# Gated DeltaNet recurrence: the decay to a chunk's end moved from the new values to two copies of the keys, with two buffers each for the keys

## The chip, the cores and the metric

One core of one Trainium2 chip. The metric is the device time of one execution in microseconds (us); the kernel before takes 2288.92 us (median of three runs, 2286.33 to 2290.3).

## The reference

A decoder trunk of two layers over 1024 tokens of width 1024, in float32: layer 0 mixes a dilated attention and a gated linear recurrence, layer 1 is a gated DeltaNet. The change lies in layer 1 alone. Its core, per head, in chunks of tokens (the reference uses 64, the kernel 128):

```python
decay  = exp(where(causal, gcum[:, None] - gcum[None, :], -inf))
sol    = triangular_solve(I + strict_lower((k*b) @ k.T * decay), [v*b, k*b*exp(gcum)])
u, w   = sol                                     # w multiplies the state
q_dec  = q * exp(gcum)
k_tail = k * exp(gcum[-1] - gcum)                # the decay to the chunk's end
g_last = exp(gcum[-1])
def step(state, n):
    v_new = u[n] - w[n] @ state
    o     = q_dec[n] @ state + (q @ k.T * decay)[n] @ v_new
    state = state * g_last[n] + k_tail[n].T @ v_new
    return state, o
```

There are 8 key heads and 16 value heads; two value heads, e = 0 and 1, share one key head and differ in `gcum`. `k` and `q` come from a projection (1024 x 1024 per group), a causal convolution of 4 taps and SiLU. The output goes through an RMS norm, a SiLU gate and an output projection.

## The kernel before, in words

The kernel is written with a framework that places semaphores, gives tiles their buffers and orders each engine's instructions itself: an instruction is put in the queue of its engine when, in the order in which the program writes things, it is the first whose operands and buffers are there. So what stands later in the program can run earlier when what stands before it waits. A tile with a tag shares `bufs` slots with all tiles of that tag; a new tile gets a slot when the last reader of the slot's tile before has run.

Layer 1 (`odd_layer`) goes through eight key heads `hh`. Each has three parts:

- *Projection* `proj(j)`: first `way_out(j - 2)`, the gates of the head before (L143 to L145 into banks named oz, output through tiles `oy`, tag "oy", 2 buffers), then four convolutions `conv`: k of head j + 1 (matmuls into banks pk), the two value heads of head j (pv), q of head j (pq). Every product of the projections is three matmuls (high and low parts). A convolution takes PSUM banks of the tag "pj" (2 banks), one for each half of the tokens. ACT copies the bank to the staging tile `ub` (L822, tag "ub", 1 buffer); then the result tile (`kT`, `vT` or `q`) is taken and written by ACT (L825), worked on by DVE three times (L827), by ACT (L830) and by DVE (L831). `kT` has the tag "kT" with 3 buffers, `q` the tag "q" with 2.
- `turn_k(j)` turns the keys by PE transposes into banks "a" and copies them to `kn` (L877, tag "kn", 3 buffers), one half by ACT, one by DVE. `turn_v` does the same for the values, scaled (`bv`).
- *Inversion* `invert(hh)`: the matrix of each chunk (kk, from `kT`) is inverted on DVE in small steps (L1007, L1009) and by small matmuls; the result is `U`.
- *Recurrence* `recur(hh)`, 8 chunks of 128 tokens, both value heads side by side (2 x 128 columns). Per chunk: `ks` = keys times state (L1105), `r` = values minus that (DVE, L1108); `qs` = queries times state (L1111), `oq` = that scaled (ACT, L1114); `vp` = U times r (L1120), the new values; `vt` = vp times the decay to the chunk's end, `etl` (DVE, L1123); `vn` = plain copy of vp (ACT, L1125); `kv` = turned keys times vt (L1129); the new state `S` (DVE, L1133); `op` = attention times vn (L1140); for the next chunk `qk` (L1091) and its masked product `A` (DVE, L1093), with decays that SP loads and POOL and ACT prepare (L1079, L1081). PSUM: tag "b" has two banks, "d" one, "c" one, "a" two. `ks`, `kv` and `op` take "b"; `qs`, `vp` and `qk` take "d".

The three parts run together. While recurrence hh runs, the inversion of hh + 1 and `proj(hh + 1)` are laid between its steps:

```python
for hh in range(8):
    fill = proj(hh + 1) if hh < 7 else seq(way_out(6), gate7(), out_last(range(3), ["pj"]))
    if hh < 7:
        fill = blend(invert(hh + 1), fill, 0.8)
    mix(recur(hh), fill, 2.8)
    drain(fill)
```

So during recurrence hh the keys `kT` of three heads are about: hh (recurrence), hh + 1 (inversion), hh + 2 (being convolved). The weights come by SP's DMAs and are cut into high and low parts by ACT and DVE (L112, L113). After the last head, the output projection adds into `hr` (L273), and `after` computes the final norm into tiles `fo` (tag "kn"; L199, L1173) and writes them out. The first group of its inputs sits in the slots of "kT" and "kn" too.

Of the kernel before, what the change touches and what calls it, by code (L numbers as in the profile page):

```python
# [9 lines left out]
F32 = mybir.dt.float32  # L10
F32R = mybir.dt.float32r
# [3 lines left out]
ALU = mybir.AluOpType  # L15
# [3 lines left out]
P = 128  # L19
D = 1024  # L20
T = 1024
NT = T // P
# [56 lines left out]
def trunk_kernel(ctx: ExitStack, tc: tile.TileContext, x, ew, ewo, ow, owab, owo, nw, fnw, lbl, hnw,  # L79
                 cw, dtb, alog, onw, cst, out):  # L80
    nc = tc.nc
    dve, act, pe, pool = nc.vector, nc.scalar, nc.tensor, nc.gpsimd
# [8 lines left out]
    def bank(tag, shape, name):  # L91
        return pp.tile(shape, F32, name=name, tag=tag, bufs=BANKS[tag])
# [647 lines left out]
    def odd_layer(es):  # L740
        sp = es.enter_context(tc.tile_pool(name="od", bufs=1))
        gt = {n: sp.tile([P, NT, 16], F32, name=f"g_{n}") for n in ("beta", "gc", "ngc", "eg", "nbeg", "etl", "egl")}
# [70 lines left out]
        KT, KN, SC, Q, BV, CQ, SS, VT, US = {}, {}, {}, {}, {}, {}, {}, {}, {}  # L813
# [32 lines left out]


        def k_tile(j):
            KT[j] = sp.tile([P, T], F32, name=f"kT{j}", tag="kT", bufs=3)
            return KT[j]  # L850

        def q_tile(j):
# [9 lines left out]
        def turn_k(j):  # L862
            ss = sp.tile([P, NT], F32, name=f"kss{j}", tag="kss", bufs=2)
            tps = turn_qk(KT[j], ss, f"tk{j}")
            rn = sp.tile([P, NT], F32, name=f"rn{j}", tag="rn", bufs=2)
            tm = sp.tile([P, NT], F32, name=f"rt{j}", tag="rt", bufs=2)
            dve.tensor_scalar(ss, ss, 4.0 * EPS, None, op0=ALU.add)
            rsqrt(rn, ss, tm)

            dve.tensor_tensor(tm, rn, rn, op=ALU.mult)  # L870
            sc = SC[j] = sp.tile([P, 3, NT, 2], F32, name=f"sc{j}", tag="sc", bufs=3)
            for i, (n, f, x) in enumerate((("beta", 1.0, tm), ("nbeg", 1.0, tm), ("beta", 0.5, rn))):
                dve.scalar_tensor_tensor(sc[:, i], gt[n][:, :, 2 * j:2 * j + 2], f, x[:, :, None].to_broadcast([P, NT, 2]),
                                         op0=ALU.mult, op1=ALU.mult)
            kn = KN[j] = sp.tile([P, NT, 128], F32, name=f"kn{j}", tag="kn", bufs=3)
            for h in range(2):
                (dve.tensor_copy if h else act.copy)(kn[:, 4 * h:4 * h + 4, :], tps[h])  # L877


        def v_tile(j, e):  # L880
# [80 lines left out]
        def decays(hh, c, w):  # L961
            g = sp.tile([P, 2, 128], F32, name=f"gc{w}{hh}_{c}", tag=f"gc{w}", bufs=2)
            nc.sync.dma_start(g, bass.AP(tensor=gcd.tensor, offset=gcd.offset + (c * 16 + 2 * hh) * 128,
                                         ap=[[0, P], [128, 2], [1, 128]]))
            return g
# [106 lines left out]
        def recur(hh):  # L1072

            kT, kn, q, bv, U = KT[hh], KN[hh], Q[hh], BV[hh], US[hh]
            ss = SS[hh] = sp.tile([P, NT, 2], F32, name=f"oss{hh}", tag="oss", bufs=2)

            def decay_a(c):
                DA = decays(hh, c, "a")
                pool.tensor_tensor(DA, DA, MA[:, None, :].to_broadcast([P, 2, 128]), op=ALU.add)  # L1079
                for e in range(2):  # L1080
                    act.activation(DA[:, e, :], DA[:, e, :], AF.Exp, bias=gt["ngc"][:, c, 2 * hh + e:2 * hh + e + 1])  # L1081
                return DA

            def attend(c):

                DA = ahead_a.pop()
                if c < NT - 1:
                    ahead_a.append(decay_a(c + 1))
                qk = bank("d", [P, 128], f"qk{hh}_{c}")
                s = slice(c * 128, (c + 1) * 128)  # L1090
                pe.matmul(qk, kT[:, s], q[:, s], start=True, stop=True)  # L1091
                A = sp.tile([P, 2, 128], F32, name=f"A{hh}_{c}", tag="A", bufs=2)
                dve.tensor_tensor(A, qk[:, None, :].to_broadcast([P, 2, 128]), DA, op=ALU.mult)  # L1093
                return A

            ahead_a = [decay_a(0)]
            yield 1.0
            A = attend(0)
            St = None
            for c in range(NT):  # L1100
                col = [slice(2 * hh + e, 2 * hh + e + 1) for e in range(2)]
                s = slice(c * 128, (c + 1) * 128)
                if c:
                    ks = bank("b", [P, 2, 128], f"ks{hh}_{c}")
                    pe.matmul(ks, kT[:, s], St, start=True, stop=True)  # L1105
                    r_ = sp.tile([P, 2, 128], F32, name=f"r{hh}_{c}", tag="r")
                    for e in range(2):
                        dve.scalar_tensor_tensor(r_[:, e, :], ks[:, e, :], SC[hh][:, 1, c, e:e + 1],  # L1108
                                                 bv[:, c, e, :], op0=ALU.mult, op1=ALU.add)
                    qs = bank("d", [P, 2, 128], f"qs{hh}_{c}")  # L1110
                    pe.matmul(qs, q[:, s], St, start=True, stop=True)  # L1111
                    oq = sp.tile([P, 2, 128], F32, name=f"oq{hh}_{c}", tag="oq")
                    for e in range(2):
                        act.activation(oq[:, e, :], qs[:, e, :], AF.Copy, scale=gt["eg"][:, c, col[e]])  # L1114
                else:
                    r_ = bv[:, 0]
                yield 1.0
                vp = bank("d", [P, 2, 128], f"vp{hh}_{c}")
                for e in range(2):
                    pe.matmul(vp[:, e, :], U[:, 2 * c + e, :], r_[:, e, :], start=True, stop=True)  # L1120
                if c < NT - 1:
                    vt = sp.tile([P, 2, 128], F32, name=f"vt{hh}_{c}", tag="vt")
                    dve.tensor_tensor(vt, vp, gt["etl"][:, c, 2 * hh:2 * hh + 2, None].to_broadcast([P, 2, 128]), op=ALU.mult)  # L1123
                vn = sp.tile([P, 2, 128], F32, name=f"vn{hh}_{c}", tag="vn")
                act.copy(vn, vp)  # L1125
                yield 1.0
                if c < NT - 1:
                    kv = bank("b", [P, 2, 128], f"kv{hh}_{c}")
                    pe.matmul(kv, kn[:, c, :], vt, start=True, stop=True)  # L1129
                    Sn = sp.tile([P, 2, 128], F32, name=f"S{hh}_{c}", tag="S", bufs=2)  # L1130
                    if c:
                        for e in range(2):
                            dve.scalar_tensor_tensor(Sn[:, e, :], St[:, e, :], gt["egl"][:, c, col[e]],  # L1133
                                                     kv[:, e, :], op0=ALU.mult, op1=ALU.add)
                    else:
                        dve.tensor_copy(Sn, kv)
                    St = Sn
                op = bank("b", [P, 2, 128], f"op{hh}_{c}")
                for e in range(2):
                    pe.matmul(op[:, e, :], A[:, e, :], vn[:, e, :], start=True, stop=True)  # L1140
                A = attend(c + 1) if c < NT - 1 else None
                if c:
                    dve.tensor_tensor(bv[:, c], op, oq, op=ALU.add)
                else:
                    dve.tensor_copy(bv[:, c], op)
                for e in range(2):
                    jk = sp.tile([P, 128], BF16, name=f"oj{hh}_{c}_{e}", tag="jk", bufs=2)
                    act.activation(jk, bv[:, c, e, :], AF.Square, accum_out=ss[:, c, e:e + 1])
                yield 1.0
# [8 lines left out]
        def y_parts(g):  # L1158
            if g:
                return y_load(*y_tile(f"lo{g % 2}", 8 + g), g * 256)  # L1160
            yh = [sp.tile([P, T], F32R, name=f"oyh{c}", tag="kT", bufs=3) for c in range(2)]
            yl = [sp.tile([P, T], F32R, name=f"oyl{c}", tag="kn", bufs=3) for c in range(2)]
            y_load(yh, yl, 0)
            for t in range(NT):
                nc.sync.dma_start(hres(t), h1[t * 128:(t + 1) * 128, :])
            return yh, yl

        def after(t):
            o = sp.tile([P, D], F32, name=f"fo{t}", tag="kn", bufs=3)
            rs = norm_stats(hres(t), f"f{t}", sp, o, 2 if t == NT - 1 else 1)  # L1170
            m = D // 2 if t == NT - 1 else D
            for n in range(0, D, m):
                dve.scalar_tensor_tensor(o[:, n:n + m], hres(t)[:, n:n + m], rs, nwf[:, n:n + m], op0=ALU.mult, op1=ALU.mult)  # L1173
                nc.sync.dma_start(out[t * 128:(t + 1) * 128, n:n + m], o[:, n:n + m])
# [95 lines left out]
```

## Time and profile before

| | us |
|---|---|
| median of three runs | 2288.92 |
| the profiled execution | 2290.27 |
| its span | 2288.5 |
| PE busy in the span | 2171.9 |
| DVE busy | 1427.0 |
| ACT busy | 963.4 |
| POOL busy | 226.5 |

Times in the profile count from the start of the span. PE is the tensor engine's matmuls, PEld its weight loads, DVE the vector engine, ACT the scalar engine, POOL the GpSimd engine, SP the engine that issues DMAs. A row of the groups names line, engine, operation, output <- inputs, shape, count, then busy us and mean ns of one, then the idle time of the engine just before these instructions and what ended most of it. A row of a window has its length, then for each engine its busy time and count, then the granted clock of PE as a share of full speed and the DMA engines' share and rate. A row of a single tile has its count, the shortest, median and longest duration in ns, and the first and the last start in us. Layer 1 lies between about 1220 and 2150 us; a float32 matmul of the program shows as two in the trace.

### The profile page before, as it was taken

How to read it: one execution, taken by the hardware profiler on the slowest of the kernel's cores; microseconds unless marked ns; L12 is line 12 of the kernel's file. 1: busy time of each engine (PE TensorE's matmuls, PEld its weight loads, DVE VectorE, ACT ScalarE, POOL GpSimd, SP SyncE). 2: the span in 40 equal slices, each digit the busy share in tenths (PEclk: the TensorE clock that was granted, in tenths of full speed). 3: DMA queues.
4: the chain of work that ended last, by engine and by line, in shares of the span. 5: the costliest groups of instructions: out<-in, count | busy, mean ns of one | idle time of the engine just before them, and what ended most of it. 6: DMA issues, size and time to landing. Idle time of an engine off the chain costs nothing. (4 is left out here: it accounts for less than half of the span.)

```text
span 2288.5 us, 54642 instructions
## 1 busy us (share of the span) xinstructions
PE 2171.9 (95%) x22597; PEld 1809.0 (79%) x22597; DVE 1427.0 (62%) x3364; ACT 963.4 (42%) x2623; POOL 226.5 (10%) x236
## 2 busy tenths in 40 slices
PE   7999999999999999988999988989899989899998
PEld 6888888898888888866887776767777767678787
DVE  6444444444444444456777887878788877855777
ACT  5333333333333332322236663755555555544223
POOL 0000000000000000000000012131212121210000
PEclk9999999999999999999999998999999999999999
DMA  4111111113222323352323221121212121214232
GB/s 145 38 48 48 44 47 48 43 39 95 78 82 84 90 83 92 97 160 88 102 97 104 59 56 62 53 79 46 76 43 76 52 74 59 65 60 148 91 113 109
DMA packets 101864, 175.83 MB, mean 77 GB/s; under 512 B 16752, under 2 KB 34032, under 8 KB 101616
## 3 DMA queue, kind: packets, MB, share of 16 engines
q1 hardware_dynamic: 101616, 172.35, 24.2%
q8 instruction: 177, 2.90, 0.5%
q14 instruction: 71, 0.58, 0.1%
HBM read 127.07 MB, written 25.23 MB: 67 GB/s over the span
## 5 line engine op out<-in xcount | busy, mean ns | idle before, releaser
L113 DVE TENSOR_TENSOR w_lo<-raww,w_hi 128x512 fp32r<-128x512 f32 x292 | 211.9, 727 | 151.1 <-ACT w_hi L112 147.1
L112 ACT CAST w_hi<-raww 128x512 fp32r<-128x512 f32 x292 | 181.1, 620 | 270.1 <-PE op L145 68.0
L143 PE MATMUL av<-w_hi,hn_hi 128*128 128x256 f32 x512 | 149.0, 291 | 0.0
L143 PE MATMUL bi<-w_hi,hn_hi 128*128 128x256 f32 x512 | 147.0, 287 | 0.0
L144 PE MATMUL bi<-w_lo,hn_hi 128*128 128x256 f32 x512 | 145.3, 284 | 0.0
L144 PE MATMUL av<-w_lo,hn_hi 128*128 128x256 f32 x512 | 144.8, 283 | 0.0
L145 PE MATMUL bi<-w_hi,hn_lo 128*128 128x256 f32 x512 | 144.8, 283 | 0.0
L145 PE MATMUL av<-w_hi,hn_lo 128*128 128x256 f32 x512 | 144.7, 283 | 0.0
L575 ACT ACTIVATE P<-P,nm 128x256 f32<-128x256 f32 (+7 forms) x128 | 71.4, 559 | 130.2 <-DVE nm L573 130.0
L143 PE MATMUL op<-w_hi,yplo 128*128 128x512 f32 x288 | 113.5, 394 | 1.6 <-DVE hr L273 0.9
L145 PE MATMUL op<-w_hi,yplo 128*128 128x512 f32 x288 | 112.2, 390 | 0.0
L144 PE MATMUL op<-w_lo,yplo 128*128 128x512 f32 x288 | 112.1, 389 | 0.0
L143 PE MATMUL pv<-hn_hi,w_hi 128*128 128x512 f32 x256 | 107.0, 418 | 2.6 <-ACT uv L822 2.6
L143 PE MATMUL oz<-hn_hi,w_hi 128*128 128x512 f32 x256 | 109.4, 427 | 0.0
L273 DVE TENSOR_TENSOR hr<-hr,op 128x512 f32<-128x512 f32 x128 | 86.1, 684 | 34.5 <-PE op L145 34.0
L145 PE MATMUL pv<-hn_hi,w_lo 128*128 128x512 f32 x256 | 104.3, 407 | 0.0
L144 PE MATMUL pv<-hn_lo,w_hi 128*128 128x512 f32 x256 | 102.6, 401 | 0.0
L144 PE MATMUL oz<-hn_lo,w_hi 128*128 128x512 f32 x256 | 102.3, 400 | 0.0
L145 PE MATMUL oz<-hn_hi,w_lo 128*128 128x512 f32 x256 | 102.0, 398 | 0.0
L581 DVE STREAM_TRANSPOSE PB<-P 128x256 f32<-128x256 f32 (+3 forms) x64 | 54.6, 854 | 74.9 <-ACT P L575 74.8
L143 PEld LDWEIGHTS av<-w_hi,hn_hi 128*128 128x128 f32 x512 | 97.9, 191 | 3.5 <-issue 1.9
L144 PEld LDWEIGHTS bi<-w_lo,hn_hi 128*128 128x128 f32 x512 | 98.1, 192 | 0.0
(354 smaller groups left out, 6044.9 us busy)
## 6 DMA issues: line engine op xcount, KB each, us to landing
raww<-in_ew_dram SPq DMA_DIRECT2D x128, 256.0 KB, 3.1
raww<-in_ow_dram SPq DMA_DIRECT2D x100, 256.0 KB, 3.0
V<-v SPq DMA_DIRECT2D x256, 64.0 KB, 2.0
rawy<-ymix SPq DMA_DIRECT2D x64, 256.0 KB, 2.7
raww<-in_ewo_dram SPq DMA_DIRECT2D x32, 256.0 KB, 3.0
gcl<-gcd SPq DMA_DIRECT2D x64, 128.0 KB, 3.0
gca<-gcd SPq DMA_DIRECT2D x64, 128.0 KB, 3.0
ymix<-oy SPq DMA_DIRECT2D x32, 256.0 KB, 2.0
```

Source lines behind the costliest of these rows:

```text
L112: act.copy(hi, raw)
L113: dve.tensor_tensor(lo, raw, hi.bitcast(F32), op=ALU.subtract)
L143: pe.matmul(ps, lh, rh, start=start, stop=False)
L144: pe.matmul(ps, lh, rl, start=False, stop=False)
L145: pe.matmul(ps, ll, rh, start=False, stop=stop)
L273: dve.tensor_tensor(dst[:, n], src[:, n], ps, op=ALU.add)
L575: act.activation(Pm[:, e, w0:], Pm[:, e, w0:], AF.Exp, bias=nmx[:, e:e + 1], scale=0.125, accum_out=den[:, i, e:e + 1])
L581: dve.transpose(PB[:, :, i * WG + w0:(i + 1) * WG], Pm[:, :, w0:])
```

## The change

The decay to the chunk's end is put on the keys instead of on the values: k_tail = etl x k for each of the two value heads. `turn_k` copies the turned keys by ACT to a tile `raw` (in the slots of "oy") and POOL multiplies it by `etl` of each value head, so that `kn` is twice as large. `vt` is no longer made, and `kv` takes `vn`, as two products of 128 columns with two weight tiles in place of one of 256. `ks` takes the bank "d" and `qs` the bank "b". The room for the larger `kn` comes from the buffers: "kT" has 2 instead of 3, "kn" 2 of twice the size instead of 3. The first inputs of the output projection and `fo` take other slots accordingly.

```diff
         def k_tile(j):
-            KT[j] = sp.tile([P, T], F32, name=f"kT{j}", tag="kT", bufs=3)
+            KT[j] = sp.tile([P, T], F32, name=f"kT{j}", tag="kT", bufs=2)
...
-            kn = KN[j] = sp.tile([P, NT, 128], F32, name=f"kn{j}", tag="kn", bufs=3)
+            kn = KN[j] = sp.tile([P, 2, NT, 128], F32, name=f"kn{j}", tag="kn", bufs=2)
             for h in range(2):
-                (dve.tensor_copy if h else act.copy)(kn[:, 4 * h:4 * h + 4, :], tps[h])
+                raw = sp.tile([P, 4, 128], F32, name=f"kr{j}_{h}", tag="oy", bufs=2)
+                act.copy(raw, tps[h])
+                for e in range(2):
+                    et = gt["etl"][:, 4 * h:4 * h + 4, 2 * j + e:2 * j + e + 1]
+                    pool.tensor_tensor(kn[:, e, 4 * h:4 * h + 4, :], raw, et.to_broadcast([P, 4, 128]), op=ALU.mult)
...
-                    ks = bank("b", [P, 2, 128], f"ks{hh}_{c}")
+                    ks = bank("d", [P, 2, 128], f"ks{hh}_{c}")
...
-                    qs = bank("d", [P, 2, 128], f"qs{hh}_{c}")
+                    qs = bank("b", [P, 2, 128], f"qs{hh}_{c}")
...
-                if c < NT - 1:
-                    vt = sp.tile([P, 2, 128], F32, name=f"vt{hh}_{c}", tag="vt")
-                    dve.tensor_tensor(vt, vp, gt["etl"][:, c, 2 * hh:2 * hh + 2, None].to_broadcast([P, 2, 128]), op=ALU.mult)
                 vn = sp.tile([P, 2, 128], F32, name=f"vn{hh}_{c}", tag="vn")
                 act.copy(vn, vp)
...
-                    pe.matmul(kv, kn[:, c, :], vt, start=True, stop=True)
+                    for e in range(2):
+                        pe.matmul(kv[:, e, :], kn[:, e, c, :], vn[:, e, :], start=True, stop=True)
...
-            yh = [sp.tile([P, T], F32R, name=f"oyh{c}", tag="kT", bufs=3) for c in range(2)]
-            yl = [sp.tile([P, T], F32R, name=f"oyl{c}", tag="kn", bufs=3) for c in range(2)]
+            yh = [sp.tile([P, T], F32R, name=f"oyh{c}", tag=t, bufs=2) for c, t in enumerate(("kT", "q"))]
+            yl_ = sp.tile([P, 2, T], F32R, name="oyl", tag="kn", bufs=2)
+            yl = [yl_[:, c, :] for c in range(2)]
...
-            o = sp.tile([P, D], F32, name=f"fo{t}", tag="kn", bufs=3)
+            o = sp.tile([P, D], F32, name=f"fo{t}", tag="kn", bufs=2)
```

## The prediction

> **What bounds the kernel now.** I read the page first, then busy time in windows of one head each, the groups by line, a few tiles in one head, and the timeline of two chunks.
>
> ```profile
> span 2288.5 us, 54642 instructions
> PE 2171.9 (95%) x22597; PEld 1809.0 (79%) x22597; DVE 1427.0 (62%) x3364; ACT 963.4 (42%) x2623; POOL 226.5 (10%) x236
> ```
> ```profile
> core 0: us, PE busy (x) PEld busy (x) DVE busy (x) ACT busy (x) POOL busy (x), PEclk, DMA share, GB/s
> 1611.00:1718.00 107.00, 99.34 (x697) 80.56 (x697) 85.02 (x227) 60.62 (x183) 21.31 (x23) 1.00 0.21 63
> 1718.00:1825.00 107.00, 99.91 (x702) 81.10 (x701) 85.56 (x226) 61.28 (x183) 21.16 (x23) 1.00 0.20 62
> 1825.00:1934.00 109.00, 99.78 (x700) 80.63 (x699) 87.36 (x229) 61.96 (x185) 21.29 (x23) 1.00 0.22 66
> ```
>
> PE is the bound. The odd layer's heads follow each other every 107 to 109 us, and PE works 99 to 100 of them; DVE has 22 us to spare per head, POOL 86. A recurrence alone is a chain of latencies: what keeps PE at 93% are the next head's projection matmuls, laid between its chunks. So the question is whether the change takes these away while a recurrence runs.
>
> **The recurrence's own edits.** Groups of the odd layer, by line, and two entries of the timeline in head 0:
>
> ```profile
> L937 POOL TENSOR_TENSOR oy<-oy,g 128x512 f32<-128x512 f32 x28 | 36.5, 1305 | 67.4 <-ACT oy L936 27.5 <-ACT gcl L978 20.2 <-DVE g L915 8.8
> L1140 PE MATMUL op<-vn,A 128*128 128x128 f32 x256 | 41.2, 283 | 12.2 <-ACT vn L1125 12.1
> L1120 PE MATMUL vp<-r,L 128*128 128x128 f32 x224 | 36.0, 281 | 12.9 <-ACT oq L1114 8.8 <-DVE r L1108 3.9
> L1093 DVE TENSOR_TENSOR A<-qk,gca 128x256 f32<-128x256 f32 x64 | 26.8, 418 | 5.0 <-PE qk L1091 4.6
> L1123 DVE TENSOR_TENSOR vt<-vp,g_etl 128x256 f32<-128x256 f32 x56 | 23.5, 419 | 23.1 <-PE vp L1120 22.2
> L1125 ACT COPY vn<-vp 128x256 f32<-128x256 f32 x64 | 23.4, 366 | 22.8 <-DVE vt L1123 18.3 <-PE vp L1120 2.9 <-DVE uq L818 1.1
> L877 DVE COPY kn<-tk 128x512 f32<-128x512 f32 x8 | 5.5, 681 | 0.0
> L877 ACT COPY kn<-tk 128x512 f32<-128x512 f32 x8 | 4.9, 612 | 0.0
> ```
> ```profile
> 1376.90 0.61 PE L1120 MATMUL vp<-r,L 128*128 128x128 f32 x4
> 1378.72 0.59 PE L1129 MATMUL kv<-vt,kn 128*128 128x256 f32 x2
> ```
>
> - *vt goes* (56 x 419 ns = 23.5 us of DVE), and kv starts from vn, a step of 366 ns on ACT. DVE isn't the bound, so the 23.5 us bring nothing by themselves. But vn stands behind vt for 18.3 of its 22.8 us of idle time, and PE waits 12.1 us for vn. If that share goes, PE gains 12.1 x 18.3 / 22.8 = 9.7 us. What is late next is ACT's queue: kv, and with it the state, now stands behind whatever ACT does before vn; at 57% load against DVE's 80% I count no loss.
> - *kv becomes two products* with two weight tiles. The nearest row is vp, two products of 128 columns already: 0.61 us against 0.59 for today's kv. 56 x 0.02 = 1 us.
> - *Banks.* vp no longer waits for oq to empty "d" (8.8 us of PE). ks takes "d" after qk instead, so it waits for A, 418 ns on DVE behind the new state. Bounds: 8.8 gained, or 56 x 0.42 = 23 lost if nothing lay between. In most chunks projection matmuls lie there, so I take the gain. Together 18.5 us over 8 heads, 2.3 per head.
> - *Two scaled copies of the keys.* Per head ACT gets a copy (612 ns), DVE loses one (681 ns), POOL gets four products of 512 columns at 1305 ns, 5.2 us beside 86 idle ones. They are first read a head later: no cost; without that cover kv of chunk 0 would come 5.2 us late, 42 us in eight heads. Their two "oy" slots are wanted again only by the output of the recurrence then running. No DMA is added or moved on SP's queue.
>
> **The buffers, which decide.** kT gets two slots instead of three, but three heads want it: while recurrence hh reads kT(hh) and the inversion kT(hh+1), the convolution wants to write kT(hh+2). Single tiles in head 3 (ks reads kT3, L825 is the first write of kT5):
>
> ```profile
> L1105 PE MATMUL ks<-S,kT x14: 377/379/455, 1627.8 to 1703.2; 128*128 128x256 f32 x14
> L825 ACT ACTIVATE kT<-uk,cws x2: 735/759/783, 1662.3 to 1668.6; 128x512 f32<-128x512 f32 x2
> L822 ACT COPY uv<-pv x2: 582/584/586, 1680.0 to 1690.6; 128x512 f32<-128x512 f32 x2
> L145 PE MATMUL pq<-hn_hi,w_lo x16: 388/391/397, 1705.7 to 1717.8; 128*128 128x512 f32 x16
> L1125 ACT COPY vn<-vp x2: 351/352/353, 1708.0 to 1729.9; 128x256 f32<-128x256 f32 x2
> ```
>
> kT5 is first written at 1662.3, kT3 last read at 1703.2. With two slots kT5 must take kT3's, 41 us later. Behind that write: the staging tile "ub" is single, so the next convolution (values, pv) can't be copied out of PSUM; "pj" has two banks, full after its two halves; then no projection matmul can be issued, the gates (oz) neither. kn has one slot less too, but kn(hh) is last read by kv of chunk 6, before ks of chunk 7: covered by kT's wait.
>
> The price here: pv's second bank is emptied at 1690.6, when one chunk remains; there PE's projections now end. A chunk with few projections between (head 0), and the convolution from L825 to its last L831 where DVE is little loaded (kT1), take:
>
> ```profile
> 1381.29 0.60 PE L1105 MATMUL ks<-S,kT 128*128 128x256 f32 x2
> 1387.59 0.60 PE L1105 MATMUL ks<-S,kT 128*128 128x256 f32 x2
> ```
> ```profile
> L825 ACT ACTIVATE kT<-uk,cws x2: 727/732/737, 1247.3 to 1249.2; 128x512 f32<-128x512 f32 x2
> L831 DVE SCALAR_TENSOR_TENSOR kT<-uk,kT x2: 685/689/693, 1253.4 to 1256.9; 128x512 f32<-128x512 f32 x2
> ```
>
> These are 6.3 us and 1256.9 + 0.7 - 1247.3 = 10.3. So kT3 is free at 1690.6 + 6.3 = 1696.9, "ub" at 1707.2, and after one copy of 0.6 PE's projections go on at 1707.8. Two convolutions are left, of 12.1 us each (pq: 1705.7 to 1717.8): 1707.8 + 24.2 = 1732.0, against 1717.8 now, 14.2 us later; the next recurrence follows 12.1 after that (1729.9 - 1717.8), as now. Off that come 2.3 for the waits above, 1 for a bare chunk that the edits shorten, and 1 of the 7.7 us that PE idles per head anyway: 9.9 a head. It strikes kT3 to kT7, five times: 50 us.
>
> kT2 is a case of its own: it is written before recurrence 0 starts.
>
> ```profile
> L825 ACT ACTIVATE kT<-uk,cws x2: 724/754/783, 1301.9 to 1308.1; 128x512 f32<-128x512 f32 x2
> L1105 PE MATMUL ks<-S,kT x14: 378/379/454, 1342.5 to 1387.8; 128*128 128x256 f32 x14
> L143 PE MATMUL oz<-hn_hi,w_hi x32: 388/397/795, 1363.3 to 1416.9; 128*128 128x512 f32 x32
> L1125 ACT COPY vn<-vp x1: 372/372/372, 1424.1 to 1424.1; 128x256 f32<-128x256 f32 x1
> ```
>
> Now it waits for the end of recurrence 0. With DVE free of three convolutions I let that start 5 us earlier (between 0 and their 18 us: 3 x (6 x 0.76 + 2 x 0.69)): first ks 1337.5, last after six bare chunks of 6.3 at 1375.3. Then 10.9 for the convolution and 24.2 for the other two: 1410.4, when the gates can start, and recurrence 1 at 1422.5, as now (1424.1). By then two of the four gate halves are undone that PE now finishes by 1416.9: 2 x 6 = 12 us late.
>
> The end: "fo" has two slots.
>
> ```profile
> 2278.11 1.28 DVE L1173 SCALAR_TENSOR_TENSOR fo<-hr,rsf,nwf 128x1024 f32<-128x1024 f32 x1
> 2281.08 0.61 ACT L199 ACTIVATE fo<-hr 128x512 f32<-128x512 f32 x1
> out_dram<-fo SPq DMA_DIRECT2D x7, 512.0 KB, 2.6
> ```
>
> The last tile's first square (2281.08) needs the slot of tile 5, written out at 2278.11 + 1.28 + 2.6 = 2282.0: 0.9 us.
>
> Sum: 50 + 12 + 1 + 1 = 64 on the profiled execution's 2290.3, which stands 1.4 above the median of 2288.9: about **2353 us** by the median.
>
> **The rivals.**
> - *Slower still: the clock falls in the holes.* A hole that the trace already has:
>
> ```profile
> 1395.00:1399.00 4.00, 0.56 (x3) 0.20 (x2) 3.93 (x13) 0.69 (x2) 2.61 (x3) 1.00 0.02 5
> 1399.00:1406.00 7.00, 4.50 (x36) 2.97 (x38) 6.63 (x13) 2.55 (x4) 4.59 (x7) 0.52 0.15 44
> 1406.00:1413.00 7.00, 7.00 (x153) 5.61 (x150) 2.52 (x4) 1.86 (x3) 5.17 (x6) 0.51 0.26 93
> ```
>
>  After 4 us with 0.56 of PE's work the granted clock is half for 14 us. Six holes of some 10 us, each followed by as much, would cost up to 6 x 7 = 42 us more: 2395, or 2405 with a second bare chunk in the stall. [...] I leave it out of the sum, since the chain after the hole is set by DVE and ACT as much as by PE.
> - *The pipeline only shifts.* The gates and the inversion fill the hole instead. For it: DVE and POOL have room, and the 288 projection matmuls of a head are the same. Against: oz needs the two "pj" banks that pv holds. If three quarters of the 9.9 and of the 12 are absorbed: 2288.9 + 15 + 2 = 2306.
> - *Faster.* The schedule puts k's convolution behind the recurrence's end without an empty PE, so that the slot is never waited for, and the 18.5 us of waits are what is left: 2288.9 - 18.5 + 2 = 2272. It decides if the other convolutions can go ahead of k's; the single "ub", taken in order, speaks against it.
> - *Nothing moves:* shift and gain cancel, 2289.
>
> **How the numbers follow.** The kT wait in each head, 0.58 (own range 2320 to 2395: 4 to 14 us a head, with or without the clock); the shift, 0.16; the clock or more above 2395, 0.07; faster, 0.11; no change, 0.08. I predict 2353. From 2286 to 2395 leaves out the faster case and the slowest, 0.18. A change of 0.2% (4.6 us) is about what a measurement of this kernel can tell from none: faster 0.11, same 0.08, slower 0.81.
>
> **What would show it.** Right: L825 for kT2 to kT7 starts after the last ks two heads before, with "ub" and the pv banks waiting behind it; a PE hole of 8 to 12 us once per head; heads 115 to 123 us apart. Also no PE wait of vp for oq, kv waiting for vn, and POOL up by some 42 us. Wrong: heads at 107 us with L825 moved but PE still at 93%, or L825 where it is now.

## The result, and the profile after

| | before, us | after, us |
|---|---|---|
| median of four runs each | 2289.61 (2286.33 to 2293.78) | 2402.45 (2397.33 to 2407.81) |
| profiled execution | 2290.27 | 2402.06 |
| its span | 2288.5 | 2400.2 |

After stands to before as 1.0489 (95% interval 1.0471 to 1.0506): 113 us slower, where 64 were predicted. The side and the place were as predicted, the size was not.

The head of the page of the kernel after:

```profile
span 2400.2 us, 54910 instructions
PE 2217.0 (92%) x22709; PEld 1844.2 (77%) x22709; DVE 1449.9 (60%) x3300; ACT 968.3 (40%) x2631; POOL 251.0 (10%) x268
```

Layer 1 and all behind it as one window, first of before, then of after (length, busy time and count of each engine, granted clock, DMA):

```profile
1210.00:2288.50 1078.50, 997.20 (x6463) 802.24 (x6461) 818.68 (x2029) 553.56 (x1577) 167.25 (x184) 0.99 0.24 74
```
```profile
1210.00:2400.20 1190.20, 1043.69 (x6581) 838.33 (x6579) 842.97 (x1969) 560.14 (x1588) 191.71 (x216) 0.95 0.23 68
```

The stretch is 111.7 us longer. PE stands idle 146.5 instead of 81.3 of it (+65.2) and is busy 46.5 longer with nearly the same work, at a lower clock. Windows of after, from one head's first `vn` to the next's, for recurrences 2 to 4:

```profile
1560.60:1683.50 122.90, 105.41 (x712) 84.97 (x712) 88.92 (x217) 61.49 (x184) 23.69 (x27) 0.96 0.19 54
1683.50:1806.50 123.00, 105.56 (x713) 85.14 (x712) 89.16 (x217) 61.65 (x185) 23.59 (x27) 0.96 0.18 54
1806.50:1931.50 125.00, 108.12 (x714) 87.13 (x712) 88.97 (x217) 61.75 (x185) 23.54 (x27) 0.92 0.18 53
```

Heads are 123 to 125 us apart instead of 107 to 109; PE idles 17 of them instead of 7 to 9. The tile of the keys during recurrence 3 (`ks` is now L1110; L825 here writes kT5):

```profile
L1110 PE MATMUL ks<-S,kT x14: 377/379/483, 1690.7 to 1756.8; 128*128 128x256 f32 x14
L825 ACT ACTIVATE kT<-uk,cws x2: 707/710/713, 1757.2 to 1757.8; 128x512 f32<-128x512 f32 x2
```

kT5 is written 0.4 us after the last read of kT3. The wait for the slot is there, as predicted. The same head in four windows: from its first `vn` to the end of the last `ks`; to the end of the first copy of pv into `ub`; to the end of pq's matmuls; to the next head's first `vn`:

```profile
1683.50:1757.10 73.60, 66.08 (x537) 52.80 (x536) 48.20 (x135) 37.98 (x125) 13.61 (x17) 1.00 0.23 68
1757.10:1764.60 7.50, 2.58 (x15) 2.18 (x15) 7.20 (x16) 4.89 (x14) 1.18 (x1) 0.85 0.07 19
1764.60:1797.90 33.30, 28.30 (x118) 22.91 (x117) 27.55 (x52) 13.51 (x37) 8.06 (x8) 0.88 0.06 20
1797.90:1806.50 8.60, 8.60 (x49) 7.25 (x47) 6.21 (x15) 5.26 (x13) 0.74 (x1) 1.00 0.34 100
```

The third is the surprise: two convolutions, for which the prediction had 24.2 us of PE, take 33.3. PE's timeline there (start, us, instructions; in brackets the idle time before and what ended it):

```profile
1759.14 0.71 PE L1143 MATMUL op<-vn,A 128*128 128x128 f32 x4 [0.52 <-ACT vn L1127]
1763.46 0.90 PE L840 MATMUL tk<-ident,kT 128*128 128x128 f32 x3 [3.61 <-DVE kT L831]
...
1774.17 0.39 PE L144 MATMUL pv<-hn_lo,w_hi 128*128 128x512 f32 x1
1779.33 1.08 PE L895 MATMUL tv<-ident,vT 128*128 128x128 f32 x4 [4.77 <-DVE vT L831]
1780.06 0.78 PE L145 MATMUL pv<-hn_hi,w_lo 128*128 128x512 f32 x1
```

The head has two holes. The first, 3.6 us, is kT5's convolution. The second, 4.8 us, lies before the transposes of the values (tv), which stand in PE's queue ahead of matmuls that could run. vT is late although its input was copied at 1764.0. DVE's timeline says why (kss, rn, rt: the norm of the keys, 8 columns):

```profile
1767.42 0.91 DVE L188 TENSOR_SCALAR rn<-kss 128x8 int32<-128x8 int32 x1
1768.37 0.96 DVE L190 SCALAR_TENSOR_TENSOR rt<-kss,rn 128x8 f32<-128x8 f32 x1
...
1773.39 0.97 DVE L192 SCALAR_TENSOR_TENSOR rn<-rt,rn 128x8 f32<-128x8 f32 x1
1774.39 0.17 DVE L190 SCALAR_TENSOR_TENSOR rt<-kss,rn 128x8 f32<-128x8 f32 x1
1774.59 0.17 DVE L191 TENSOR_TENSOR rt<-rt,rn 128x8 f32<-128x8 f32 x1
1774.68 0.74 DVE L827 SCALAR_TENSOR_TENSOR vT<-uv,cws,vT 128x512 f32<-128x512 f32 x1
```

and POOL's, in the same microseconds:

```profile
1766.27 4.03 POOL L933 TENSOR_TENSOR bv<-bv,ors 128x512 f32<-128x512 f32 x4 [5.67 <-DVE ors L192]
1770.26 4.07 POOL L882 TENSOR_TENSOR kn<-kr,g_etl 128x512 f32<-128x512 f32 x4
```

Operations of 0.17 us take 0.91 to 0.97 here while POOL works on products of 1.0 us each, one DVE operation to one product. Seven of them, 6.7 us in all instead of 1.2, lie ahead of vT's first L827. L933 is in the kernel before, too (there L928), where it ran at another time; L882 is the change's own.

### The profile page after: what moved, and what is told of

Read it like the earlier page. It is cut to its first block, busy times and chain, and to the rows that moved or that the text cites. A ratio compares the mean times of both kernels' runs of the same rounds, so it can differ in the third digit from the quotient of the medians.

```text
span 2400.2 us, 54910 instructions
## 1 busy us (share of the span) xinstructions
PE 2217.0 (92%) x22709; PEld 1844.2 (77%) x22709; DVE 1449.9 (60%) x3300; ACT 968.3 (40%) x2631; POOL 251.0 (10%) x268
## 5 line engine op out<-in xcount | busy, mean ns | idle before, releaser
L143 PE MATMUL pv<-hn_hi,w_hi 128*128 128x512 f32 x256 | 113.0, 441 | 3.0 <-ACT uv L822 2.9
L145 PE MATMUL pv<-hn_hi,w_lo 128*128 128x512 f32 x256 | 109.8, 429 | 0.0
L1084 POOL TENSOR_TENSOR gca<-gca,MA 128x256 f32<-128x256 f32 x64 | 51.0, 797 | 556.8 <-DMA gca<-gcd 436.8
L144 PE MATMUL pv<-hn_lo,w_hi 128*128 128x512 f32 x256 | 108.9, 426 | 0.0
L273 DVE TENSOR_TENSOR hr<-hr,op 128x512 f32<-128x512 f32 x128 | 86.3, 685 | 35.9 <-PE op L145 35.6
```

Source lines behind the costliest of these rows:

```text
L143: pe.matmul(ps, lh, rh, start=start, stop=False)
L144: pe.matmul(ps, lh, rl, start=False, stop=False)
L145: pe.matmul(ps, ll, rh, start=False, stop=stop)
L273: dve.tensor_tensor(dst[:, n], src[:, n], ps, op=ALU.add)
```

## The experiments

All stand beside runs of the kernel before on the same chip (medians 2289.6 to 2292.5); the ratio is to those.

**The slot alone, and the slot given back.** `a_kt2` is the kernel before with two slots for the keys; of the rest of the change it has only what this forces, another slot for one input of the output projection.

```diff
-            KT[j] = sp.tile([P, T], F32, name=f"kT{j}", tag="kT", bufs=3)
+            KT[j] = sp.tile([P, T], F32, name=f"kT{j}", tag="kT", bufs=2)
...
-            yh = [sp.tile([P, T], F32R, name=f"oyh{c}", tag="kT", bufs=3) for c in range(2)]
+            yh = [sp.tile([P, T], F32R, name=f"oyh{c}", tag=t, bufs=2) for c, t in enumerate(("kT", "q"))]
```

> The kernel before with one edit: the keys kT have two slots instead of three (the second high input tile of the output projection moves to a slot of q). Everything else, vt, the banks and three kn slots, is as before. Theory S (the missing third kT slot makes nearly all of the 112 us): 2385 to 2405 us, heads 121 to 125 us apart, the first write of kT2 to kT7 (L825) within 1 us after the last ks two heads before. Rival R (the recurrence's own edits, POOL's products or the second kv product slow it): 2289 to 2305 us, and L825 hardly waits.

Measured 2407.69 us (2398.62 to 2409.54), ratio 1.0492 (1.0467 to 1.0517), 3 us above the range of theory S, with heads 1 to 5 lasting 123 to 129 us. The slot alone makes as large a loss as the whole change. `c_kt3` is the reverse, all of the change with a third slot; the room comes from `kn` without the last chunk, which `kv` never reads, and from smaller temporaries.

```diff
-            KT[j] = sp.tile([P, T], F32, name=f"kT{j}", tag="kT", bufs=2)
+            KT[j] = sp.tile([P, T], F32, name=f"kT{j}", tag="kT", bufs=3)
-            kn = KN[j] = sp.tile([P, 2, NT, 128], F32, name=f"kn{j}", tag="kn", bufs=2)
+            kn = KN[j] = sp.tile([P, 2, NT - 1, 128], F32, name=f"kn{j}", tag="kn", bufs=2)
...
```

> The changed kernel with a third kT slot. The room for it comes from the scaled keys (7 of 8 chunks are kept, since the last one feeds no state), one temporary of the gates in a shared slot and single scratch tiles. Theory S: the heads go back to 105 to 108 us and the time is at or below the kernel before, 2268 to 2292 us; what lies below 2289 is what the recurrence's own edits are worth (18.5 us by the prediction). Rival R: it stays above 2350 us.

Measured 2307.56 (2301.27 to 2312.13), ratio 1.0067 (1.0045 to 1.0089). Nearly all of the loss is gone, but 16 us remain, so the time misses theory S (2292 at most): the recurrence's own edits, for which I had counted 18.5 us of gain, lose. The smaller temporaries are in this kernel too, and no run has them alone; ACT's operations on the scratch tiles show no cost (those on `oj` 39.2 us busy and 72.5 idle before them, in the kernel before 38.4 and 74.6).

**Which waits cost how much.** `l_k2free` is the kernel before with two slots, where kT2 has a third of its own, so that only kT5, kT6 and kT7 wait; in `m_k2only` kT2 alone waits.

```diff
+ l_k2free: tag="kTx" if j == 2 else "kT", bufs=1 if j == 2 else 2
+ m_k2only: tag="kTa" if j in (0, 2, 5) else "kT", bufs=1 if j in (0, 2, 5) else 2
```

> The kernel before with two kT slots, but kT2 in a slot of its own, so that only kT5, kT6 and kT7 must wait for the recurrence two heads before (kT3 and kT4 find the slots of kT0 and kT1 free). Theory P (a waiting head costs 14 to 18 us each and nothing else): 2289 + 3 x 16 = 2331 to 2345 us, with heads 1 and 2 as before. Rival L (the first head that waits costs more than the others, whichever it is, since the projections lose a lead): 2350 to 2370 us.

> The kernel before, three kT slots, but kT0, kT2 and kT5 share one, so that only kT2 must wait (for recurrence 0). The prediction's step: 12 us for this head, 2301 us. Theory L (the projections of head 1 lose the lead that they have over the recurrences while the first inversion runs; in the changed kernel the first vn of heads 1 and 2 came 13 and 46 us later): 2318 to 2337 us. If the later heads make the loss good, since they wait for nothing: 2289 to 2300 us.

Measured 2338.94 (2337.27 to 2346.65), ratio 1.0212 (1.0187 to 1.0237): 47.4 us for three heads, 15.8 each. And 2321.44 (2319.27 to 2323.99), ratio 1.0129 (1.0110 to 1.0149): 29.9 for kT2 (theories P and L). With five waiting heads, 5 x 15.8 + 29.9 = 109 of the 113. The two terms of my sum were 9.9 and 12. What kT2 does to recurrence 0, before and in `m_k2only`:

```profile
1327.00:1396.00 69.00, 61.48 (x455) 49.05 (x455) 57.11 (x169) 40.63 (x122) 6.03 (x9) 1.00 0.22 58
```
```profile
1327.00:1396.00 69.00, 48.44 (x180) 34.12 (x179) 43.57 (x135) 34.38 (x119) 5.60 (x8) 0.63 0.12 33
```

The recurrence runs bare, that is, with few projection matmuls between its steps: 180 matmuls instead of 455, and the clock falls to 0.63.

**The staging tile.** `g_ub2` is the kernel after with a second `ub`; the room comes from `kn` and the temporaries, as in `c_kt3`.

```diff
-            ub = sp.tile([P, T + 3], F32, name=f"u{name}", tag="ub")
+            ub = sp.tile([P, T + 3], F32, name=f"u{name}", tag="ub", bufs=2)
...
```

> The changed kernel, two kT slots, with a second staging tile ub (room from the scaled keys of the last chunk, which feed no state, and scratch tiles). The value convolution can then be emptied and worked on while kT's write waits, and 48 more projection matmuls can be issued. Theory S with the single ub as the stopper: heads 110 to 116 us apart, 2320 to 2355 us. Rival (only kT's own slot counts, whatever stands behind it): 2385 to 2405 us.

Measured 2332.73 (2332.60 to 2334.24), ratio 1.0180 (1.0162 to 1.0198): some 71 of the 113 us come back, though the keys still wait for their slot. Heads 2 to 5 last 5.4 us longer than before on average, with one `ub` 15.8: most of the price of a waiting head is what the wait closes behind it. Another 23 us arise once, between the first `vn` of head 1 and that of head 2.

**The order of the convolutions.** `j_order` puts the first convolution of the values ahead of the keys', so that it no longer stands behind the slot.

```diff
+            yield from conv(w, 1, 16 + 2 * j, f"v{j}_0", lambda: v_tile(j, 0), late)
...
-            yield from conv(w, 1, 16 + 2 * j, f"v{j}_0", lambda: v_tile(j, 0), ...)
```

> The changed kernel, two kT slots, but the convolution of the next keys but one is put behind the first value convolution instead of ahead of it (the turning of queries, values and keys moves with it). So 48 more projection matmuls can go before the wait for kT, some 12 us of PE. Theory S with the single staging tile and two full pj banks as the stopper: the hole shrinks by 8 to 12 us in each of six heads, 2320 to 2350 us. Rival O (the stall is set by what comes after kT's release, the order ahead of it does not matter): 2385 to 2405 us.

Measured 2392.11 (2388.15 to 2396.82), ratio 1.0438 (1.0420 to 1.0456): 12 us back, far less than theory S had, and in the range of rival O. The last `ks` now comes 83 us after the first `vn` instead of 73 to 74, the hole behind it is 2.6 to 2.8 us, and the one before tv stays, 4.6 to 6.5. The move shifted the work and took neither hole away.

**Filling the holes.** `f_warm` and `f2_warm` add matmuls whose result nobody reads, to keep PE busy in the holes.

```diff
+ f_warm:  wk = bank("c", [P, 512], f"wk{j}"); 5 x pe.matmul(wk, ident, KT[j + 1][:, 0:512], ...)
+ f2_warm: wm = bank("b", [P, 2, 128], f"wm{hh}"); 8 x pe.matmul(wm, ident, vn, ...)   # last chunk
```

> The changed kernel with PE kept busy in its two holes per head: seven matmuls of 256 columns after the last vn of heads 0 to 5, and five of 512 columns on the new kT behind the second value convolution, into a bank that nobody reads; they are extra work, the output is unchanged. After this the granted clock should hardly fall in the steady heads (five heads with 10 to 20 us at half speed each in the changed kernel). Theory H (the lower clock after a hole costs time on the path): 5 to 7 us less per head, 2365 to 2380 us. Rival D (DVE and ACT set the pace after a hole, the clock is beside the path): 2398 to 2415 us, with the clock near 1.00 in these heads.

> The changed kernel with eight extra matmuls of 256 columns after the last vn of heads 0 to 5, into a bank of the tag b that nobody reads; extra work, the output is unchanged. They should lie in the hole of 3.6 us behind the last chunk, which the first try with bank c missed (its matmuls ran 37 us later). Theory H (half clock after this hole is on the path): the stretch at half speed behind it goes, 3 us less per head, 2380 to 2392 us. Rival D (the matmuls behind the hole end ahead of DVE anyway, a later hole of 4.8 us waits for DVE): 2397 to 2412 us, that later hole longer by some 3 us.

`f_warm`: 2444.57 (2440.56 to 2446.30), ratio 1.0664 (1.0648 to 1.0680); its matmuls came some 37 us late and missed the holes, so it tells nothing. `f2_warm`: 2419.22 (2415.06 to 2431.82), ratio 1.0550 (1.0523 to 1.0576). They lay in the first hole, but the second went from 4.7 to 5.9 us in heads 1 to 5 to 3.7 to 7.3, and the mean clock hardly changed (0.967 to 0.977 in the four runs, in after 0.967 to 0.974). Both runs lie above the ranges of both theories. That the clock behind the first hole sets the pace isn't borne out; it isn't excluded either, since the clock still fell and the added work moved the rest.

**POOL's products.** `n_dve` is the kernel after with the key products on DVE; `s_nopool` has L933, the scaling of `bv`, on DVE as well.

```diff
-                    pool.tensor_tensor(kn[:, e, 4 * h:4 * h + 4, :], raw, ...)
+                    dve.tensor_tensor(kn[:, e, 4 * h:4 * h + 4, :], raw, ...)
... s_nopool only:
-                pool.tensor_tensor(bv[:, t:t + 2], bv[:, t:t + 2], ...)
+                dve.tensor_tensor(bv[:, t:t + 2], bv[:, t:t + 2], ...)
```

> The kernel after, with one edit: the products that scale the turned keys (4 of 512 columns per head) run on DVE instead of POOL. Theory: POOL's products, 1.0 us each, hold back DVE's small operations of the inversion (128x8: 0.17 us alone, 0.9 to 1.0 us while a product runs), so the values' convolution comes late and the turned values with it, and PE stands 4.7 us before them; with the products on DVE (4 of about 0.7 us = 3 us a head) the small operations take 0.17 us again, that hole shrinks below 3 us, and a head gains 3 to 6 us: 2365 to 2385 us. Rival: POOL lies beside the path and DVE only gets 3 us more work a head: 2398 to 2410 us, hole unchanged.

> The kernel after with both large products (the scaled keys and the scaling of bv, 4 of 512 columns a head each) on DVE instead of POOL. Theory (POOL holds DVE's 128x8 steps): they take 0.17 us throughout, the hole before the turned values falls below 2 us, and the time comes 3 to 15 us under the run with the key products alone on DVE (2381 us): 2366 to 2378. Rival: what is left is the chain of the convolution itself, and DVE's 3 us more a head eat the gain: 2378 to 2390.

Measured 2381.40 (2379.26 to 2389.43), ratio 1.0398 (1.0373 to 1.0422), and 2371.12 (2370.02 to 2378.45), ratio 1.0351 (1.0333 to 1.0369): 21 and 31 us back, both in the range of the theory, with more work on DVE. The group of the transposes tv, of after, `n_dve` and `s_nopool` in turn (busy and mean, then PE's idle time before them):

```profile
L895 PE MATMUL tv<-ident,vT 128*128 128x128 f32 x128 | 22.9, 312 | 30.7 <-DVE vT L831 28.6 <-DVE Tp L1014 1.3 <-DVE uq L818 0.9
```
```profile
L895 PE MATMUL tv<-ident,vT 128*128 128x128 f32 x128 | 20.8, 288 | 14.5 <-DVE vT L831 13.1 <-DVE ors L192 1.4
```
```profile
L895 PE MATMUL tv<-ident,vT 128*128 128x128 f32 x128 | 19.7, 278 | 3.3 <-DVE vT L831 1.9 <-DVE ors L192 1.4
```

PE's wait for vT goes from 28.6 to 13.1 to 1.9 us. The third of the four windows, again of `n_dve` and of `s_nopool`:

```profile
1755.40:1783.40 28.00, 25.53 (x118) 20.68 (x117) 24.81 (x55) 12.97 (x36) 4.56 (x4) 0.96 0.06 20
```
```profile
1759.90:1786.10 26.20, 25.56 (x118) 20.47 (x118) 24.65 (x59) 12.85 (x36) 0.00 (x0) 0.97 0.08 26
```

33.3, 28.0 and 26.2 us for the same 118 matmuls, with 8.06, 4.56 and 0 us of POOL in them; the clock goes from 0.88 to 0.97. In head 3 of `n_dve` three of the 8-column operations beside the remaining L933 still take 0.91 to 1.00 us; in that of `s_nopool` all of them take 0.15 to 0.16.

**The recurrence's own edits.** `d_banks` is the kernel before with the bank exchange alone.

```diff
-                    ks = bank("b", [P, 2, 128], f"ks{hh}_{c}")
+                    ks = bank("d", [P, 2, 128], f"ks{hh}_{c}")
-                    qs = bank("d", [P, 2, 128], f"qs{hh}_{c}")
+                    qs = bank("b", [P, 2, 128], f"qs{hh}_{c}")
```

> The kernel before with the bank exchange alone: ks takes d, qs takes b. As the prediction had it: vp no longer waits for oq (8.8 us of PE) and ks is covered by projection products, 2276 to 2285 us. Rival, from c_kt3's waits: ks now waits for A, which DVE makes behind the new state, and qs waits for the state in ks's old place: 2290 to 2302 us, with a wait of ks for A of 4 to 8 us in the groups.

Measured 2302.40 (2299.03 to 2310.77), ratio 1.0061 (1.0040 to 1.0082): a loss of 10 us by the medians, 14 by the ratio, as the rival had it. A group of the kernel before, and four of this one:

```profile
L1105 PE MATMUL ks<-S,kT 128*128 128x256 f32 x112 | 34.6, 390 | 10.3 <-DVE S L1133 8.7 <-DVE Tp L1009 1.5
```

```profile
L1140 PE MATMUL op<-vn,A 128*128 128x128 f32 x256 | 41.6, 285 | 13.2 <-ACT vn L1125 13.2
L1120 PE MATMUL vp<-r,L 128*128 128x128 f32 x224 | 36.8, 289 | 6.1 <-DVE r L1108 6.1
L1105 PE MATMUL ks<-S,kT 128*128 128x256 f32 x112 | 34.6, 390 | 4.5 <-DVE A L1093 4.5
L1111 PE MATMUL qs<-S,q 128*128 128x256 f32 x112 | 34.3, 388 | 12.6 <-DVE S L1133 10.6 <-DVE Tp L1009 2.0
```

The 8.8 us of `vp` for `oq` are gone, as predicted, and come back elsewhere: `ks` waits 4.5 for `A`, and the wait for the new state moved from `ks` (8.7 before) to `qs` (10.6); `vp` waits 6.1 for `r` instead of 3.9. The chain from state to state got no shorter. `o_kt3dve` is `c_kt3` with the key products on DVE, and `p_best` gives the tail back too:

```diff
-            o = sp.tile([P, D], F32, name=f"fo{t}", tag="kn", bufs=2)
+            o = sp.tile([P, D], F32, name=f"fo{t}", tag="kn" if t % 2 else "kT", bufs=2 if t % 2 else 3)
```

> The kernel with a third slot for the keys (c_kt3), with the same edit: key products on DVE. Theory: of the 16 us by which c_kt3 is above the kernel before, a part comes from POOL's products beside DVE's steps of the recurrence and the inversion: 2278 to 2296 us, vn of chunk 0 to ks of chunk 1 nearer to 5 us than to 7.2. Rival: it comes from the recurrence's own chain (kv behind vn on ACT, ks behind A, qs behind S), whichever engine scales the keys: 2300 to 2310 us, and PE's waits for S before qs, A before ks and vn before kv stay at about 20 us in all.

> o_kt3dve, and the tail given back: the tiles of the final norm alternate between the slots of the turned keys and of the keys, so that the last ones no longer wait for an output transfer. The theory of the tail (two slots cost 2.5 to 3.3 us at the end): 2 to 4 us below o_kt3dve, and no wait of the last tiles for the transfer of an earlier one. Rival (the end is set by the output projection): same as o_kt3dve within 1 us.

`o_kt3dve`: 2315.39 (2309.48 to 2315.65), ratio 1.0098 (1.0078 to 1.0117): no gain. The waits are the rival's (S before qs 7.0, A before ks 5.6, vn before kv 9.1 us, 21.7 in all), the time lies 5 us above its range. With a third slot, then, the move brings nothing; whether POOL's products cost nothing there or DVE's extra work eats the gain stays open. `p_best`: 2309.87 (2306.58 to 2312.35), ratio 1.0078 (1.0061 to 1.0095): 5.5 below `o_kt3dve` by the medians, more than the 2 to 4 expected, with overlapping runs; no `fo` waits for a transfer any more. Two versions without the exchange: `q_nobank` (three slots, the tail as in `p_best`, POOL's products), and `r_vndve`, where DVE makes `vn` in the place that `vt` had.

```diff
+ q_nobank: ks = bank("b", ...); qs = bank("d", ...)     # as in the kernel before
- act.copy(vn, vp)
+ dve.tensor_copy(vn, vp)                                # r_vndve, added to q_nobank
```

> The kernel with a third slot for the keys (c_kt3), the bank exchange undone (ks in b, qs in d, as before), and the final norm's tiles alternating over two tags. What is left of the change is vt's removal and the scaled keys. Theory: c_kt3's 16 us over the kernel before are the exchange (14 us by itself) and the tail (2 to 3): 2287 to 2297 us, vp waits for oq again (about 9 us) and op waits less for vn. Rival: the chain over ACT (kv behind vn) costs as well: 2298 to 2308.

> q_nobank with the copy of the new values made by DVE, in the place where the kernel before made vt, instead of by ACT. The work per chunk is then the kernel before's without ACT's copy and without its wait behind vt (18.3 of 22.8 us). Theory: PE's 12.1 us of waits of op for vn go and kv starts as early as before: 2276 to 2287, below both kernels. Rival: DVE is the later of the two engines, and vn waits in its queue behind the inversion's steps: 2290 to 2300.

`q_nobank`: 2307.75 (2303.28 to 2309.32), ratio 1.0066 (1.0052 to 1.0080); `r_vndve`: 2303.16 (2301.04 to 2307.43), ratio 1.0048 (1.0034 to 1.0062). Both miss the theory. The first lies in the range of its rival, but not for the rival's reason, as `kv` waits only 2.6 us for `vn`; the second lies above its rival's range as well. In `q_nobank` the removal of `vt` does what it should to `op`, which waits 0.8 us instead of 12.1, yet the time doesn't follow:

```profile
L1145 PE MATMUL op<-vn,A 128*128 128x128 f32 x256 | 39.3, 275 | 0.8 <-ACT vn L1129 0.8
L1127 PE MATMUL vp<-r,L 128*128 128x128 f32 x224 | 37.1, 288 | 17.0 <-ACT oq L1121 9.9 <-DVE r L1115 7.1
L1112 PE MATMUL ks<-S,kT 128*128 128x256 f32 x112 | 36.3, 406 | 11.2 <-DVE S L1138 11.1
```

The waits for `r`, `S` and `oq` grew by 3.2, 2.4 and 1.1 us. Layer 1 and all behind it, of `c_kt3` and of `q_nobank`, to set beside before's 1078.50 us with 997.20 of PE:

```profile
1210.00:2299.40 1089.40, 994.54 (x6556) 806.31 (x6555) 813.05 (x1961) 562.75 (x1581) 204.27 (x216) 0.99 0.24 73
```
```profile
1210.00:2305.20 1095.20, 1008.69 (x6578) 815.82 (x6576) 814.63 (x1967) 564.52 (x1585) 203.06 (x216) 0.98 0.24 74
```

In these executions the two lose in different ways. `c_kt3` is 10.9 us longer, with PE idle 13.6 more and busy 2.7 less: its loss is waits. `q_nobank` is 16.7 longer, with PE idle only 5.2 more and busy 11.5 longer, and part of that is clock. A stretch of recurrence 3 in `q_nobank`, in the inversion's small matmuls:

```profile
1676.00:1684.00 8.00, 5.79 (x177) 4.53 (x176) 7.76 (x14) 2.12 (x4) 4.16 (x6) 1.00 0.13 38
1684.00:1688.00 4.00, 4.00 (x11) 3.13 (x11) 2.77 (x7) 2.32 (x9) 0.73 (x1) 0.57 0.39 102
```

Recurrences 3 and 4 have a clock of 0.98 in `q_nobank`, 1.00 in the kernel before. 4 us at 0.57 cost 4 x 0.43 = 1.7 at most, so one such drop in each of the two makes no more than 3.4 of the 16.7 us, by this estimate. No version beats the kernel before.

**What a second staging tile leaves.** `t_ub2dvenb` is `g_ub2` with the exchange undone and the key products on DVE.

> The kernel after with a second staging tile (g_ub2, 2333 us), with the bank exchange undone and the key products on DVE; two slots for the keys stay. Theory: the 41 us that were left are the exchange (up to 14), POOL's products (5 to 15) and the one lead lost ahead of the first recurrence (some 20 to 30, which a second staging tile does not give back): 2305 to 2322 us. Rival: the slot wait alone still costs 6 us a head, and the two edits lie in its shadow: 2325 to 2336.

Measured 2325.60 (2321.14 to 2328.49), ratio 1.0144 (1.0127 to 1.0160), just inside the rival's range: the two edits give some 7 us. By the first `vn` of each head against before, 22 us arise once, between heads 1 and 2, and 1.6 to 6.4 in each of the next four heads (4 on average).

## Why the prediction was wrong in size

**The wait and its place: right.** Groups of PE and one of POOL in after:

```profile
L1143 PE MATMUL op<-vn,A 128*128 128x128 f32 x256 | 42.2, 290 | 4.7 <-ACT vn L1127 4.7
L1125 PE MATMUL vp<-r,L 128*128 128x128 f32 x224 | 39.1, 295 | 22.8 <-DVE r L1113 21.5 <-DVE Tp L1014 1.3
L1132 PE MATMUL kv<-vn,kn 128*128 128x128 f32 x224 | 38.7, 297 | 14.5 <-ACT vn L1127 14.5
```
```profile
L882 POOL TENSOR_TENSOR kn<-kr,g_etl 128x512 f32<-128x512 f32 x32 | 34.2, 1099 | 192.7 <-ACT g_etl L804 184.3 <-ACT kr L879 8.4
```

kT2 to kT7 are each written within 0.8 us of the last `ks` two heads before; `op` waits 4.7 us for `vn` instead of 12.1, `kv` now waits for it (14.5), no `vp` waits for `oq` (but 21.5 us for `r`, before 3.9). The hole of 8 to 12 us is two, 3.6 and 4.8. Heads lie 123 to 125 us apart where I gave 115 to 123. POOL is up 24.5 us, not 42: its key products take 1.10 us, not 1.305, and other groups less than before (the scaling of `bv` 1.04 us, before 1.25).

**A waiting head: 9.9 predicted, 15.8 measured.** My steps against the four windows of head 3:

| step | predicted, us | after | `s_nopool` |
|---|---|---|---|
| first `vn` to the slot free | 74.0 | 73.6 | 73.5 |
| keys' convolution and one copy | 10.9 | 7.5 | 7.4 |
| two convolutions (pv, pq) | 24.2 | 33.3 | 26.2 |
| pq's end to the next `vn` | 12.1 | 8.6 | 9.0 |
| credits (waits 2.3, chunk 1, idle 1) | -4.3 | none beside these | none |
| sum | 116.9 | 123.0 | 116.1 |

The step that failed is "POOL gets four products of 512 columns at 1305 ns, 5.2 us beside 86 idle ones. They are first read a head later: no cost", and with it "Two convolutions are left, of 12.1 us each", which let PE set the pace. In the stall the values' convolution on DVE is the path, and POOL's products, the change's and those of L933, hold back the DVE operations ahead of it. With all of them on DVE this step takes 26.2 instead of 33.3. Heads 2 to 5 last longer than before by 15.8 us on average in after, by 11.9 in `n_dve` and by 10.0 in `s_nopool`. What I had not asked is whom a busy POOL slows.

So my 9.9 would have held but for POOL's products, though partly by luck: in `s_nopool` the keys' convolution is 3.5 and the way to the next `vn` 3.1 us shorter than I had, the two convolutions are 2.0 longer, and the credits of 4.3 don't appear as a term of their own. `a_kt2`, which lacks the change's edits and L882, shows that the edits do help in the stall; the first three windows of its head 3:

```profile
1688.40:1769.60 81.20, 70.80 (x520) 55.53 (x518) 49.44 (x139) 34.53 (x113) 13.12 (x17) 0.92 0.21 59
1769.60:1781.40 11.80, 6.20 (x26) 5.02 (x26) 9.53 (x26) 8.04 (x34) 2.70 (x3) 0.63 0.05 13
1781.40:1809.00 27.60, 26.35 (x113) 21.42 (x114) 24.27 (x51) 14.48 (x31) 2.28 (x3) 0.91 0.13 40
```

In its heads 2 to 5 the first two steps take 75 to 81 and 11 to 12 us, in after 73 to 75 and 7.5; the third takes 27.3 to 27.6, in after 33.3 to 34.4. The edits gained about what POOL's products then lost, which is why `a_kt2` and after agree. With three slots the 18.5 us of gain became a loss of 11 to 22 in five versions.

**kT2: 12 predicted, 30 measured.** In after the last `ks` of recurrence 0 starts at 1381.3, where I had it at 1375.3, and from the first copy (1392.6) to pq's end it takes 35.6 us instead of 24.2:

```profile
1392.60:1428.20 35.60, 32.63 (x338) 25.22 (x339) 32.23 (x79) 14.36 (x30) 12.22 (x15) 0.94 0.09 27
```

So the gates start at 1428.8, not 1410.4: 18 us, on top of my 12; 6 of them are recurrence 0's later end, 11 this stretch. The step that failed is again the 24.2 "for the other two": 224 of these 338 matmuls are the inversion's of head 1 (`up`, `qp`, `q`, `u`), which I had left out of this stretch. It isn't POOL's key products: `m_k2only`, which has none, takes 33.8 us there. What sets the pace in it I haven't shown.

**The clock.** I left it out of the sum, as the case "slower still" with up to 42 us. The 46.5 us of longer busy time are mostly that, by an estimate from the two windows (0.95 over layer 1 and what follows, before 0.99: 997.2 x 0.99 / 0.95 = 1039 of the 1043.7 us). In `s_nopool` the second hole went and the half clock behind it went too (0.88 to 0.97); whether the half clock costs time of its own beside the wait ahead of it, no run separates. The range of the likeliest should have had it in. In head 3 of after it is 0.50 from 1763 to 1769, at the end of the hole of 3.6 us and behind it, and from 1780 to 1782, behind that of 4.8; the matmuls of pv come every 0.43 us there (1766.08 to 1768.64), every 0.23 at 1.00 (1772.13 to 1774.17). In `q_nobank` it falls at 1684 with no gap in the 8 us before longer than 1.31 us, only 5.79 of them busy. What makes it fall, no run shows.

**The tail: 0.9 predicted, 3.1 measured.** ACT's last squares in after, and the last addition into `hr`:

```profile
2389.10 0.69 DVE L273 TENSOR_TENSOR hr<-hr,op 128x512 f32<-128x512 f32 x1
2391.22 1.06 ACT L199 ACTIVATE fo<-hr 128x1024 f32<-128x1024 f32 x1 [2.85 <-DMA out_dram<-fo]
2393.72 0.63 ACT L199 ACTIVATE fo<-hr 128x512 f32<-128x512 f32 x1 [1.02 <-DMA out_dram<-fo]
```

I had one wait, of the last tile. The tile before it waits for a transfer too, so that the last one comes later as well. From the last addition's end (2389.8) to the end of the span it is 10.4 us; in the kernel before it is 7.2, without such a wait.

With the measured sizes the sum closes: 5 x 15.8 + 30 + 3 = 112. Of the 49 us that my sum lacks, 5 x 5.9 = 29 lie in the waiting heads, 18 in kT2 and 2 in the tail.

**Open.** Why, with three slots and without the exchange, what is left of the change (no `vt`, two `kv` products, the scaled keys, and the smaller temporaries) costs 11 to 15 us: the exchange alone costs 10 to 14, both together 16, so they don't add, and I have only the moved waits, PE's longer busy time and the drops of the clock, no run that separates them. A third slot with both of POOL's products on DVE wasn't tried.

## What to carry to other kernels

A buffer taken from a tile that three stages want costs more than its wait: find what stands behind it in order (here one staging tile, two PSUM banks) and cost that chain on every engine in it, not only on the one that bounds the kernel. An engine with idle time is no free place for work if its instructions slow a neighbour (here DVE's operations of 0.17 us took 0.91 to 0.97 beside POOL's products); look at the neighbour's smallest operations beside it. And a wait taken out of a chain that goes from state to state is a gain only if the whole chain gets shorter: count the waits that take its place.

## What the hardware showed

- In head 3 of after, seven of the eight DVE operations on 128x8 elements beside POOL's 128x512 products of 1.0 us (1766.27 to 1774.33) took 0.91 to 0.97 us, one to each product; the eighth, L867, took 0.17, and the next four, behind the products, 0.16 to 0.17. L190 to L192 read two tiles and L188 one. In head 3 of `s_nopool`, with no product on POOL there, all took 0.15 to 0.16. What couples the two engines, no run here shows.
- In `q_nobank` the clock stood at 0.57 over 4 us (1684 to 1688), with no PE gap over 1.31 us in the 8 us before, of which PE was busy 5.79, in part with matmuls of 32x32.
